# Order of the first loads, layout of the pool weights and turns of the memory rows in the opening of an eight-core decoder step

## The chip, the cores and the metric

The kernel runs on the 8 cores of one Trainium2 chip, every core with its own prompt sequence and 16 sample rows. The metric is the device time of the slowest core in microseconds (us). Some executions fall into a slower state, in which the cores of one die or both show a lower mean granted TensorE clock (in e1 a run of 1730.86 us with 0.93 to 0.94 on one die, and one of 1887.69 us with 0.93 to 0.95 on one and 0.84 to 0.85 on the other; 0.989 or more on every core in every fast run); only fast runs are compared. A ratio below is the mean time of one kernel's fast runs over that of the kernel before's fast runs of the same rounds, so it is not quite the ratio of the medians that stand beside it.

In this kernel TensorE (PE) does the matrix products into eight PSUM banks, VectorE (DVE), ScalarE (ACT) and GpSimd (POOL) the elementwise work. SyncE (SP) and GpSimd issue the loads, each on a queue of its own (59.24 and 84.08 MB on the page of the kernel before).

## The reference, cut to what matters

```python
def trunk(x, ...):                                   # DEPTH = 2
    for i in range(2):
        u = rmsnorm(x, g_mix[i])
        y = pool_mixer(u, ...) if i == 0 else conv_mixer(u, ...)
        x = x + y
        x = x + mem_attend(rmsnorm(x, g_attn[i]), mem_k[i], mem_v[i], w_q[i], w_o[i])
        x = x + sq_relu_mlp(rmsnorm(x, g_ffn[i]), w_up[i], w_down[i])
# pool_mixer: mean over a trailing window minus the token, one 256x256 product per group, a channel scale
# mem_kv: k, v = split(rmsnorm(mem, g_mem) @ w_kv)      256 memory rows per sequence
```

## The kernel before

The kernel keeps its own scheduler: operations are written in program order, each engine executes its own in that order, and semaphores come from the overlaps of buffers. The change sits in the `prelude`, the opening: it loads 16 blocks of x (128 rows, 512 KB each, seven buffers), applies the pool mixer and transposes x into the resident array `X`, and also turns the memory rows and multiplies them with w_k.

```python
xload(0); dma(SP, GV2, gv); xload(1)                       # SyncE's queue
dma(POOL, SCB, gv[R_PSCALE].broadcast_to([128, D]), "wpf") # GpSimd's queue: the pool scale on 128 partitions
dma(POOL, BANDS, bands)
for cc in range(2):
    dma(POOL, WPF[cc], w_pool[:, cc*128:(cc+1)*128, :].rearrange("g p e -> p g e"), "wpf")   # 1 KB rows
xload(2); dma(SP, MR, mem) ...; xload(3..6)
dma(POOL, SK, w_k); dma(POOL, SQ_, w_q)

def poolw():                                   # step 1
    8 x stt(WP(cc, g), WPF[cc](g), gain, SCB(g))              # VectorE, for the prompt
    2 x tt(WPS(cc), WPF[cc](), SCB(), mult, eng=POOL)         # GpSimd, a second copy for the samples
def stA(tb):  sum of squares of block tb on ACT; rstd; tsc(u, xrow(tb), rstd)   # normalise, DVE
def stB(tb):  window sums on PE; two copies out of PSUM, one on DVE, one on ACT
def stC(tb):  transpose of x and the pool product on PE; two copies into X
              if tb + 7 < 16: xload(tb + 7)               # SyncE: reuse of the buffer
def mem_turn(k):  one bank: 4 transposes; ACT copy, DVE copy, ACT copy, DVE copy of that bank
    if k == 3:
        dma(SP, memn, MEMN1)                              # spill of the turned memory rows
        dma(SP, GBC, gv[R_MIX].broadcast_to([128, D]))    # overwrites the bytes of MEMN1
# step s runs stB(s-1), stC(s-2), stA(s+1), then: poolw in step 1, mem_stats in step 2,
# mem_turn in steps 3 and 4, the four products rows(w_k) in steps 9 to 12
...
def attn_phase(l):
    bank_mod[0] = 7          # bank 7 is set aside; nxt() gives bank_ctr % bank_mod, the counter just goes on
```

The softmax here doesn't subtract the row's maximum and nothing guards it: scores larger than these inputs give would overflow.

## Time and profile before

| | us |
|---|---|
| time, median of 4 runs | 1642.3 (1640.96 to 1643.0) |
| opening, mean of the 8 cores | 101.1 (99.9 to 102.3) |
| rest, mean of the 8 cores | 1533.8 (1532.2 to 1535.1) |

"Opening" is read from the trace of each core: from the span's start to TensorE's transposes of the sample rows (16x16 f32). "Rest" is the span less the opening.

The page of the kernel before, slowest core (4): the span, TensorE's busy time, and the share of each engine in the chain that ended last.

```profile
span 1636.1 us, 28409 instructions; the slowest of 8 cores (1633.4 to 1636.1 us)
PE 1577.5 (96%) x10088; PEld 907.1 (55%) x10104; DVE 848.6 (52%) x1899; ACT 563.0 (34%) x1062; POOL 114.6 (7%) x245
PE 90%; DVE 3%; DMA 3%; ACT 2%; issue 2%; POOL 0%; DVEq 0%; ACTq 0%; SPq 0%; POOLq 0%
```

TensorE is nearly always busy, so what can be won lies where it is not. The chain of waits of the opening, same core (start, length, what):

```profile
3.56 17.97 DMA MEM<-w_pool
...
47.61 7.92 DMA memn<-MEM
55.59 0.33 SPq L354
56.08 10.31 DMA MEM<-x
```

There are two stalls on loads: for the pool weights until 21.5 us, and from 47.6 to 66.4 us for an x block whose issue stood in SyncE's queue behind the gain broadcast, which waited for the spill. The timeline between them (start, busy time, engine, line, operation, count):

```profile
21.62 7.42 DVE L327 SCALAR_TENSOR_TENSOR MEM<-MEM 128x256 bf16<-128x256 f32 x8 [1.43 <-DMA MEM<-w_pool]
21.68 5.11 POOL L331 TENSOR_TENSOR MEM<-MEM 128x1024 bf16<-128x1024 f32 x2 [15.54 <-DMA MEM<-w_pool]
```

The eight gain products and GpSimd's second copy run side by side.

The wait of 3.6 us ends at 990.6 us, where the second attention phase begins:

```profile
989.87 0.57 DVE L331 TENSOR_TENSOR MEM<-PS,MEM 128x400 bf16<-128x400 f32 x1
...
990.60 15.73 PE L292 MATMUL PS<-MEM 128*128 128x416 bf16 x75 [3.56 <-DVE MEM L331]
```

### The profile page before, as it was taken

How to read it: one execution, taken by the hardware profiler on the slowest of the kernel's cores; microseconds unless marked ns; L12 is line 12 of the kernel's file. 1: busy time of each engine (PE TensorE's matmuls, PEld its weight loads, DVE VectorE, ACT ScalarE, POOL GpSimd, SP SyncE). 2: the span in 40 equal slices, each digit the busy share in tenths (PEclk: the TensorE clock that was granted, in tenths of full speed). 3: DMA queues.
4: the chain of work that ended last, by engine and by line, in shares of the span. 5: the costliest groups of instructions: out<-in, count | busy, mean ns of one | idle time of the engine just before them, and what ended most of it. 6: DMA issues, size and time to landing. Idle time of an engine off the chain costs nothing.

```text
span 1636.1 us, 28409 instructions; the slowest of 8 cores (1633.4 to 1636.1 us)
## 1 busy us (share of the span) xinstructions
PE 1577.5 (96%) x10088; PEld 907.1 (55%) x10104; DVE 848.6 (52%) x1899; ACT 563.0 (34%) x1062; POOL 114.6 (7%) x245
## 2 busy tenths in 40 slices
PE   3899999999999999999999998999999999999997
PEld 3675555555555556555555554555555555555565
DVE  4566675555444344445666664676555444442235
ACT  3666344532111222222123223443652111213453
POOL 2002120110000000000000001120110000000000
PEclk9899999999999999999999999999999999999999
DMA  9859795675648617077000009694764773000012
GB/s 232 208 84 158 159 169 100 117 140 80 89 65 128 102 28 104 3 101 108 1 1 1 1 1 149 122 190 109 120 126 60 109 104 52 14 1 1 39 65 105
DMA packets 84565, 145.13 MB, mean 89 GB/s; under 512 B 4286, under 2 KB 37310, under 8 KB 84412
## 3 DMA queue, kind: packets, MB, share of 16 engines
q0 software_dynamic: 67568, 84.08, 38.0%
q1 hardware_dynamic: 16860, 59.24, 11.2%
q8 instruction: 84, 1.38, 0.3%
q14 instruction: 53, 0.43, 0.1%
HBM read 212.42 MB, written 14.36 MB: 139 GB/s over the span
## 4 chain that ended last, share of the span: by engine, by line
PE 90%; DVE 3%; DMA 3%; ACT 2%; issue 2%; POOL 0%; DVEq 0%; ACTq 0%; SPq 0%; POOLq 0%
PE PS L292 88%; DVE MEM L327 2%; PE PS L296 2%; ACT MEM L319 1%; DMA MEM<-w_pool 1%; PE PS L301 1%; DMA MEM<-x 1%; ACT MEM L308 1%; DMA memn<-MEM 0%; DVE MEM L345 0%; DVE MEM L331 0%; DMA y<-MEM 0%; DVE MEM L339 0%; ACT MEM L343 0%; POOL MEM L354 0%
## 5 line engine op out<-in xcount | busy, mean ns | idle before, releaser
L292 PE MATMUL PS<-MEM 128*128 128x416 bf16 (+7 forms) x9008 | 1502.0, 327 | 11.1 <-DVE MEM L331 4.6
L292 PEld LDWEIGHTS PS<-MEM 128*128 128x128 bf16 (+1 forms) x9024 | 837.2, 98 | 663.6 <-issue 44.0
L319 ACT ACTIVATE MEM<-PS 128x416 f32<-128x416 f32 (+5 forms) x469 | 238.7, 510 | 639.0 <-PE PS L292 628.4
L331 DVE TENSOR_TENSOR MEM<-PS,MEM 128x416 f32<-128x416 f32 (+6 forms) x533 | 297.5, 574 | 268.6 <-PE PS L292 260.5
L331 DVE TENSOR_TENSOR MEM<-MEM 128x416 bf16<-128x416 f32 (+3 forms) x282 | 159.8, 583 | 198.8 <-ACT MEM L319 190.3
L327 DVE SCALAR_TENSOR_TENSOR MEM<-MEM 128x416 bf16<-128x416 f32 (+7 forms) x322 | 181.1, 614 | 127.4 <-ACT MEM L319 102.1
L319 ACT ACTIVATE MEM<-MEM 128x416 bf16<-128x416 f32 (+9 forms) x299 | 185.1, 630 | 146.9 <-DVE MEM L331 112.2
L304 DVE SCALAR_TENSOR_TENSOR MEM<-MEM,PS 128x256 f32<-128x256 f32 x256 | 105.1, 420 | 72.6 <-PE PS L292 48.9
L296 PE MATMUL PS<-MEM 128*128 128x128 bf16 (+4 forms) x896 | 64.0, 252 | 26.8 <-DVE MEM L327 8.9
L343 ACT COPY MEM<-PS 128x512 f32<-128x512 f32 (+3 forms) x73 | 39.2, 537 | 130.9 <-PE PS L292 116.9
L296 PEld LDWEIGHTS PS<-MEM 128*128 128x128 bf16 (+2 forms) x896 | 51.2, 109 | 41.9 <-issue 40.3
L343 ACT CAST MEM<-PS 128x512 bf16<-128x512 f32 (+2 forms) x73 | 39.7, 556 | 65.9 <-PE PS L292 64.5
L345 DVE CAST MEM<-PS 128x512 bf16<-128x512 f32 (+1 forms) x68 | 43.8, 655 | 11.5 <-PE PS L292 11.3
L354 POOL DMA_DIRECT2D MEM<-cv x64 | 47.6, 744 | 13.8 <-PE PS L292 13.8
L319 ACT ACTIVATE PS<-PS 128x416 f32<-128x416 f32 (+3 forms) x67 | 33.1, 494 | 41.5 <-PE PS L292 41.2
L327 DVE SCALAR_TENSOR_TENSOR MEM<-PS,MEM 128x1024 f32<-128x1024 f32 (+1 forms) x17 | 21.8, 1282 | 44.9 <-ACT MEM L319 42.6
L351 POOL MEMSET MEM<- 128x4 bf16 (+1 forms) x96 | 15.0, 159 | 359.0 <-PE PS L296 271.7
L301 PE MATMUL PS<-MEM 128*128 128x128 f32 (+5 forms) x184 | 23.7, 268 | 14.3 <-DMA MEM<-gv 9.0
L339 DVE TENSOR_SCALAR MEM<-MEM 128x1024 bf16<-128x1024 f32 (+1 forms) x18 | 13.5, 753 | 32.9 <-ACT MEM L319 32.9
L354 POOL DMA_DIRECT2D MEM<-w_up x36 | 20.6, 581 | 137.9 <-PE PS L292 137.9
L301 PEld LDWEIGHTS PS<-MEM 128*128 128x128 f32 (+5 forms) x184 | 19.9, 139 | 16.9 <-issue 15.4
L354 POOL DMA_DIRECT2D MEM<-w_down x22 | 13.8, 636 | 201.9 <-PE PS L292 157.8
(28 smaller groups left out, 138.0 us busy)
## 6 DMA issues: line engine op xcount, KB each, us to landing
MEM<-ck SPq DMA_DIRECT2D x64, 512.0 KB, 6.9
MEM<-cv POOLq DMA_DIRECT2D x64, 256.0 KB, 6.7
MEM<-w_down POOLq DMA_DIRECT2D x6, 2048.0 KB, 18.1
MEM<-x SPq DMA_DIRECT2D x16, 512.0 KB, 11.5
MEM<-w_kv POOLq DMA_DIRECT2D x4, 2048.0 KB, 19.2
MEM<-w_o POOLq DMA_DIRECT2D x4, 2048.0 KB, 24.1
MEM<-w_up POOLq DMA_DIRECT2D x32, 256.0 KB, 12.7
MEM<-w_up POOLq DMA_DIRECT2D x4, 2048.0 KB, 17.8
```

The lines of the kernel that those rows point to most:

```text
L292: P.add(PE, "c", lambda e, o=out.ap, l=lhsT.ap, r=rhs.ap: e.matmul(out=o, lhsT=l, rhs=r, start=start, stop=stop), [lhsT, rhs], [out])
L296: P.add(PE, "c", lambda e, o=out.ap, l=lhsT.ap, r=rhs.ap: e.matmul(out=o, lhsT=l, rhs=r, start=start, stop=stop, is_transpose=is_transpose ...
L301: P.add(PE, "c", lambda e, o=out.ap, i=in_.ap, d=ident.ap: e.transpose(out=o, in_=i, identity=d), [in_, ident], [out])
L304: P.add(DVE, "c", lambda e, o=out.ap, a=in0.ap, b=in1.ap, c=acc.ap: e.scalar_tensor_tensor(out=o, in0=a, scalar=1.0, in1=b, op0=ALU.mult, ...
L308: P.add(ACT, "c", lambda e, o=out.ap, i=in_.ap, a=acc.ap: e.activation(out=o, in_=i, func=AF.Square, accum_out=a), [in_], [out, acc])
L319: P.add(ACT, "c", lambda e, o=out.ap, i=in_.ap: e.activation(out=o, in_=i, func=func, bias=bias, scale=sc), rd, [out])
L327: P.add(eng, "c", lambda e, o=out.ap, a=in0.ap, b=in1.ap: e.scalar_tensor_tensor(out=o, in0=a, scalar=sc, in1=b, op0=op0, op1=op1), rd, [out])
L331: P.add(eng, "c", lambda e, o=out.ap, a=in0.ap, b=in1.ap: e.tensor_tensor(out=o, in0=a, in1=b, op=op), [in0, in1], [out])
L343: P.add(ACT, "c", lambda e, o=out.ap, i=in_.ap: e.copy(out=o, in_=i), [in_], [out])
L345: P.add(eng, "c", lambda e, o=out.ap, i=in_.ap: e.tensor_copy(out=o, in_=i), [in_], [out])
L351: P.add(eng, "c", lambda e, o=out.ap: e.memset(o, val), [], [out])
L354: return P.add(q, "d", lambda e, o=out.ap, i=in_.ap: e.dma_start(out=o, in_=i), [in_], [out], chan=chan, after=after)
```

## The change

Its intent: the first microseconds carry only what is used first, no load waits behind another's spill (7.6 us of wait in SyncE's queue before), and ScalarE and VectorE do not wait for one bank (ScalarE waits 3.9 us, in four waits, for VectorE's copies before).

```diff
-wpool_d = din("w_pool", [4, 256, 256])
+wpool_d = din("w_pool", [2, 128, D])                     # laid out by the host: rows of 4 KB
-dma(POOL, SCB, scale row) first; bands; w_pool
+bands; w_pool in 4 KB rows; dma(POOL, SCB, scale row) last
+xload(3) ahead of the memory rows
-dma(POOL, SK, w_k); dma(POOL, SQ_, w_q)                  # at the start
+def weights():                                           # step 3, after stA(4)
+    dma(POOL, SK, w_k, after=(P.last[ACT],))
+def poolws():                                            # step 7, but next in GpSimd's own order
+    2 x tt(WPS(cc), WPF[cc](), SCB(), mult, eng=POOL); dma(POOL, SQ_, w_q); sample state
 stB:
-    second copy: eng=ACT
+    second copy: eng=ACT in odd blocks, DVE in even ones
 stC:
+    if tb == 11: dma(SP, GBC, gain row)                  # no longer behind the spill in mem_turn
-mem_turn(k): one bank, steps 3 and 4 (mem_stats in step 2)
+mem_turn(half): two banks, ACT on one while DVE is on the other, steps 4 and 5 (mem_stats in step 3)
-rows("wk0") in steps 9 to 12, their turns in 13 and 14
+rows("wk0") in steps 12 to 15, their turns in 16 and 17
 attn_phase:
+bank_ctr[0] = bank_ctr[0] % 8 % 7
 bank_mod[0] = 7
... (the sample rows scaled in place)
```

More of the change, by code (lines that the diff above doesn't have):

```diff
@@ L504, in prelude @@
         xload(1)
-        dma(POOL, SCB(), DV(gv_d[R_PSCALE:R_PSCALE + 1, :].broadcast_to([128, D])), "wpf")
         dma(POOL, BANDS(), DV(bands_d), "wp")
         for cc in range(2):
-            dma(POOL, WPF[cc](), DV(wpool_d[:, cc * 128:(cc + 1) * 128, :].rearrange("g p e -> p g e")), "wpf")
+            dma(POOL, WPF[cc](), DV(wpool_d[cc].rearrange("p (g e) -> p g e", g=4)), "wpf")
+        dma(POOL, SCB(), DV(gv_d[R_PSCALE:R_PSCALE + 1, :].broadcast_to([128, D])), "wpf")
         xload(2)
+        xload(3)
         for nb in range(2):
             dma(SP, MR[nb](), DV(mem_d[nb * 128:(nb + 1) * 128, :]), "mr")
-        for tb in range(3, NXB):
+        for tb in range(4, NXB):
             xload(tb)
-        dma(POOL, SK(), DV(wsrc_sq(wsrc["wk0"])), f"w{slot_of['wk0']}")
-        dma(POOL, SQ_(), DV(wsrc_sq(wsrc["wq0"])), f"w{slot_of['wq0']}")
         cp(IDB(), IDF())
@@ L527, in poolw @@
                     stt(WP(cc, g), WPF[cc](g), G(2 * g + cc, sl(R_MIX, R_MIX + 1)), SCB(g), ALU.mult, ALU.mult)
+        def weights():
+            dma(POOL, SK(), DV(wsrc_sq(wsrc["wk0"])), f"w{slot_of['wk0']}", after=(P.last[ACT],))
+        def poolws():
             for cc in range(2):
                 tt(WPS(cc), WPF[cc](), SCB(), ALU.mult, eng=POOL)
+            dma(POOL, SQ_(), DV(wsrc_sq(wsrc["wq0"])), f"w{slot_of['wq0']}")
             for i in range(2):
@@ L559, in stB @@
             for half in range(2):
-                cp(PLB[tb % 2](sl(half * 4, half * 4 + 4)), PSr(bks[half], "p (j t) -> p j t", j=4), eng=(ACT if half else DVE))
+                cp(PLB[tb % 2](sl(half * 4, half * 4 + 4)), PSr(bks[half], "p (j t) -> p j t", j=4), eng=(ACT if half and tb % 2 else DVE))
         def stC(tb):
@@ L578, in stC @@
                 xload(tb + NXB)
-            if tb == 10:
+            if tb == 11:
+                dma(SP, GBC(), DV(gv_d[R_MIX:R_MIX + 1, :].broadcast_to([128, D])), "gbc")
                 dma(SP, XSR(p=(0, NS)), DV(xs_d), "xsr")
@@ L589, in mem_stats, with mem_turn @@
                 tsc(MR[nb](), MR[nb](), st_(2, 16 + nb), ALU.mult)
-        def mem_turn(k):
-            bk = nxt()
-            for j in range(2):
-                c = 2 * k + j
-                for nb in range(2):
-                    tp(PSv(bk, j * 256 + nb * 128, j * 256 + (nb + 1) * 128), MR[nb](sl(c * 128, (c + 1) * 128)), IDF())
-            for j in range(2):
-                c = 2 * k + j
-                act(MEMN(c), PSv(bk, j * 256, (j + 1) * 256), AF.Copy, scale=G(c, sl(R_MEM, R_MEM + 1)))
-                tsc(MEMN1(c), PSv(bk, j * 256, (j + 1) * 256), G(c, sl(R_MEM + 1, R_MEM + 2)), ALU.mult)
-            if k == 3:
+        def mem_turn(half):
+            bks = [nxt(), nxt()]
+            for i in range(2):
+                for j in range(2):
+                    c = 4 * half + 2 * i + j
+                    for nb in range(2):
+                        tp(PSv(bks[i], j * 256 + nb * 128, j * 256 + (nb + 1) * 128), MR[nb](sl(c * 128, (c + 1) * 128)), IDF())
+            for i in range(2):
+                for j in range(2):
+                    c = 4 * half + 2 * i + j
+                    act(MEMN(c), PSv(bks[i], j * 256, (j + 1) * 256), AF.Copy, scale=G(c, sl(R_MEM, R_MEM + 1)))
+                for j in range(2):
+                    c = 4 * half + 2 * (1 - i) + j
+                    tsc(MEMN1(c), PSv(bks[1 - i], j * 256, (j + 1) * 256), G(c, sl(R_MEM + 1, R_MEM + 2)), ALU.mult)
+            if half == 1:
                 spill.append(dma(SP, DV(memn_d), V(MEMN1.ap.rearrange("p c n -> p (c n)"), MEMN1().ivs), "spill"))
-                dma(SP, GBC(), DV(gv_d[R_MIX:R_MIX + 1, :].broadcast_to([128, D])), "gbc")
         st_ctr = [0]
@@ L661, in samples_a @@
             rstd(18, P16)
-            stt(UF(p=P16), XSR(p=P16), st_(2, 18, P16), GBC(p=P16), ALU.mult, ALU.mult)
-            cp(UCB(p=P16), UF(p=P16))
-            dma(SP, DV(nps_d[:, 14, :]), UF(p=P16), "ucf")
+            stt(XSR(p=P16), XSR(p=P16), st_(2, 18, P16), GBC(p=P16), ALU.mult, ALU.mult)
+            cp(UCB(p=P16), XSR(p=P16))
+            dma(SP, DV(nps_d[:, 14, :]), XSR(p=P16), "ucf")
         def samples_b():
@@ L691, in prelude @@
         extra[1] = [poolw]
-        extra[2] = [mem_stats]
-        extra[3] = [lambda: mem_turn(0), lambda: mem_turn(1)]
-        extra[4] = [lambda: mem_turn(2), lambda: mem_turn(3)]
+        extra[3] = [weights, mem_stats]
+        extra[4] = [lambda: mem_turn(0)]
+        extra[5] = [lambda: mem_turn(1)]
+        extra[7] = [poolws]
         for i, a in enumerate(quad):
-            extra[9 + i].append(lambda a=a: rows("wk0", mk_d, *a))
+            extra[12 + i].append(lambda a=a: rows("wk0", mk_d, *a))
         for i, a in enumerate(quad):
-            extra[13 + i // 2].append(lambda a=a: turn(*a))
+            extra[16 + i // 2].append(lambda a=a: turn(*a))
         extra[11].append(lambda: norm_a(0, BUF[0], parts=2))
@@ L1455 @@
         "gv": gv, "ident": np.eye(128, dtype=np.float32), "bands": _make_bands(),
-        "w_pool": f(w_pool)[0], "w_conv_in": f(w_conv_in)[0], "w_conv_out": f(w_conv_out)[0],
+        "w_pool": f(f(w_pool)[0].reshape(4, 2, 128, 256).transpose(1, 2, 0, 3).reshape(2, 128, D)), "w_conv_in": f(w_conv_in)[0], "w_conv_out": f(w_conv_out)[0],
         "w_q": f(w_q), "w_qT": f(np.swapaxes(np.asarray(w_q), 1, 2)), "w_kv": f(w_kv), "w_o": f(w_o), "w_up": f(w_up), "w_down": f(w_down),
```

## The prediction

> **What bounds the kernel now.** The page: span 1636.1 us, TensorE busy 96%, matmuls 90% of the chain that ended last. From 101.5 us on (timeline, core 4; about 100.5 to 103 on the eight cores) TensorE is nearly always busy, so everything after that instant should only shift. The change touches what lies before it, the opening, where TensorE is busy for about 65 of 101 us. The chain of waits there shows three stalls:
> 1. 3.6 to 21.6 us: waiting for w_pool. Its two DMAs land 15 and 18 us after issue, sharing the DMA engines with x, the memory rows, w_k and w_q. The 16 engines are busy without a gap from about 3 to 72 us.
> 2. 21.6 to 29 us: the eight 128x256 gain products take 994 ns each on VectorE while GpSimd makes its second copy (2 x 2573 ns). VectorE's 128x416 form takes 644 ns, a 1024-wide one 1283 ns; from these I estimate 480 ns without company. [...]
> 3. 47.6 to 66.5 us: the DMA queue of SyncE waits 7.9 us for the spill of memn, because the gain broadcast behind it overwrites the same bytes; x blocks 10 to 14 sit behind, and ScalarE idles 6.6 us until block 10 lands (60 to 66.5 us).
> Besides, the memory transposes' copies alternate between ScalarE and VectorE on one bank: steps 3 and 4 take 12.4 us for two, where later steps take 2.6 to 4.
>
> **What the change does.**
> - Holding w_k (and w_q behind it), 4 KB rows, and the broadcast last: the first 20 us carry only what is used first. I estimate w_pool and its scale landing near 16 to 17 us instead of 21.6, the products done near 20 instead of 29: about 8 us.
> - Second copy after w_k's issue: included above. It then slows VectorE for 5 us near 26 to 31 us, where ScalarE is the limit: at most 1 us.
> - Gain broadcast issued after block 11: stall 3 goes, 6 us.
> - Two-bank memory turns: about 3 us.
> - Pool copies of even blocks moved to VectorE: ScalarE loses 0.58 us in every second step where it is the limit: about 2 us.
> Against this, the weights start near 25 us instead of 5. w_kv alone takes 18.7 us to land later in the trace, w_q the same; with the x blocks beside them I expect w_k near 50 to 53 us (first use moved to step 12, near 58) and w_q near 70 to 80, against first use near 82. So the margin for w_q is thin and may eat 0 to 4 us.
>
> **Sum.** 8 + 6 + 3 + 2 - 1 = 18, all on the chain, none given back later: continuous TensorE work starts near 83 us. 1642.4 - 18.4 = **1624 us**, range **1617 to 1632**. That is 1.1%: faster by over 2% 0.01, within 2% 0.98, slower 0.01.
>
> **What would show it.** First gain product near 17 us, each near 0.48 us; no wait of x loads on memn; w_k landing before its rows need it; TensorE continuous from 80 to 88 us; equal span from there to the end (about 1534 us).
>
> **What would make it wrong.** (a) w_q not landed when the weight transposes begin: the chain shows a wait on w_q and the gain shrinks to 10 to 14. (b) x blocks 7 to 15 land late while they share the engines with w_k and w_q: ScalarE waits on x in steps 6 to 12. (c) SyncE and GpSimd loads share the engines evenly, so the pool loads come no earlier than now. (d) w_v, issued earlier, collides with w_q's tail.

The sum: it came to 18 us (8 + 6 + 3 + 2 - 1), and the author took 18.4 us off.

## More of the kernel before

Last, who TensorE waited for after the opening (total us, times, longest):

```profile
PE PS L292 <- DVE MEM L331: 4.6, 2, 3.6
PE PS L301 <- DVE MEM L331: 4.5, 2, 3.3
```

## The result, and the profile after

The kernel after takes 1626.1 us (median of 4 runs, 1625.64 to 1626.76) against 1642.3; the ratio is 0.9903, 95% interval 0.9885 to 0.992. That is within 2%, inside the predicted range and 2 us from the predicted time. Its inner parts, however, are not the predicted ones:

| mean of 8 cores, us | before | after | difference | predicted |
|---|---|---|---|---|
| opening | 101.1 | 92.4 | 8.7 | 18.4 |
| rest | 1533.8 | 1529.1 | 4.7 | 0 |

The opening won half of what was forecast, and a place that the prediction had called untouched won 4.7 us. The two sum to 13.4 us here. The mean core span over all fast runs of a later set on one chip (the rounds of e9) fell by 14.8 us (1635.8 to 1621.0), the slowest core's by 15.5.

The page after, slowest core (5):

```profile
span 1624.3 us, 28431 instructions; the slowest of 8 cores (1618.2 to 1624.3 us)
PE 1575.0 (97%) x10104; PEld 906.3 (56%) x10104; DVE 854.2 (53%) x1907; ACT 560.8 (35%) x1054; POOL 113.9 (7%) x245
PE 92%; DVE 2%; ACT 2%; DMA 2%; issue 2%; POOL 0%; DVEq 0%; ACTq 0%; SPq 0%; POOLq 0%
```

The chain of the opening after (the scale row is `gv`):

```profile
3.31 16.70 DMA MEM<-gv
...
47.22 13.68 DMA MEM<-x
...
72.33 2.46 PE PS L296 x40
74.79 1.73 PE PS L292 x8
76.52 2.46 PE PS L296 x40
78.97 1.73 PE PS L292 x8
```

The first stall is still there, only that it is the scale that lands last, at 20.0 us. The wait for memn is gone, but x is still waited for, until 60.9 us. At the end each step is TensorE's own: 40 products of a block and 8 of a memory row, 4.2 us together. The timeline of the part between:

```profile
20.10 3.26 DVE L327 SCALAR_TENSOR_TENSOR MEM<-MEM 128x256 bf16<-128x256 f32 x8 [1.60 <-DMA MEM<-gv]
29.62 0.90 POOL L354 DMA_DIRECT2D MEM<-w_kv  x1 [25.76 <-ACT MEM L319]
30.52 4.66 POOL L331 TENSOR_TENSOR MEM<-MEM 128x1024 bf16<-128x1024 f32 x2
30.86 5.86 DVE L339 TENSOR_SCALAR MEM<-MEM 128x1024 f32<-128x1024 f32 x2 [0.88 <-ACT MEM L319]
35.89 0.45 PE L301 MATMUL PS<-MEM 128*128 128x128 f32 x1 [5.81 <-DVE MEM L339]
```

The gain products now take 3.26 us instead of 7.42. But GpSimd's second copy meets the normalisation of the memory rows: two VectorE instructions take 5.86 us, and TensorE waits 5.81 us for them. The waits of TensorE after the opening:

```profile
PE PS L301 <- DVE MEM L331: 2.4, 1, 2.4
PE PS L292 <- DVE MEM L331: 2.0, 2, 1.0
```

Where the opening's time was won and lost shows when ScalarE starts on each x block (mean of 8 cores, us, from the traces):

| block | 3 | 5 | 6 | 7 | 9 | 10 | 11 | 13 | 15 | sample transposes |
|---|---|---|---|---|---|---|---|---|---|---|
| before | 28.4 | 40.7 | 46.7 | 49.3 | 54.9 | 66.8 | 69.9 | 80.7 | 88.0 | 101.1 |
| after | 23.5 | 33.4 | 41.9 | 47.5 | 52.6 | 55.1 | 60.0 | 69.5 | 76.9 | 92.4 |
| won so far | 4.9 | 7.3 | 4.8 | 1.8 | 2.3 | 11.7 | 9.9 | 11.2 | 11.1 | 8.7 |

Some 5 us are won by block 3. Block 5's lead of 7.3 us flatters, for before had started its memory turns by then; when both kernels have them behind (blocks 7 to 9) only about 2 us are left. Then before meets its stall and the lead becomes 11.7 us, and 3 us of that are lost again toward the end.

### The profile page after: what moved, and what is told of

Same layout as the page of the kernel before. It is cut to its first block, busy times and chain, and to the rows that moved or that the text cites. A ratio compares the mean times of both kernels' runs of the same rounds, so it can differ in the third digit from the quotient of the medians.

```text
span 1624.3 us, 28431 instructions; the slowest of 8 cores (1618.2 to 1624.3 us)
## 1 busy us (share of the span) xinstructions
PE 1575.0 (97%) x10104; PEld 906.3 (56%) x10104; DVE 854.2 (53%) x1907; ACT 560.8 (35%) x1054; POOL 113.9 (7%) x245
## 4 chain that ended last, share of the span: by engine, by line
PE 92%; DVE 2%; ACT 2%; DMA 2%; issue 2%; POOL 0%; DVEq 0%; ACTq 0%; SPq 0%; POOLq 0%
PE PS L292 89%; PE PS L296 2%; DVE MEM L327 1%; ACT MEM L319 1%; PE PS L301 1%; DMA MEM<-gv 1%; DMA MEM<-x 1%; ACT MEM L308 1%; DVE MEM L331 0%; DVE MEM L345 0%; DVE MEM L339 0%; POOL MEM L354 0%; ACT MEM L343 0%; DVEq L1389 0%; ACTq L1389 0%
## 5 line engine op out<-in xcount | busy, mean ns | idle before, releaser
L292 PE MATMUL PS<-MEM 128*128 128x416 bf16 (+7 forms) x9024 | 1501.3, 327 | 8.3 <-DVE MEM L345 2.7
L292 PEld LDWEIGHTS PS<-MEM 128*128 128x128 bf16 (+1 forms) x9024 | 837.3, 98 | 659.8 <-issue 38.5
L327 DVE SCALAR_TENSOR_TENSOR MEM<-MEM 128x416 bf16<-128x416 f32 (+7 forms) x322 | 176.9, 601 | 126.9 <-ACT MEM L319 108.5
L296 PEld LDWEIGHTS PS<-MEM 128*128 128x128 bf16 (+2 forms) x896 | 49.2, 107 | 30.2 <-issue 28.6
L343 ACT CAST MEM<-PS 128x512 bf16<-128x512 f32 (+2 forms) x65 | 35.2, 554 | 68.0 <-PE PS L292 67.3
L345 DVE CAST MEM<-PS 128x512 bf16<-128x512 f32 (+1 forms) x76 | 48.5, 658 | 11.7 <-PE PS L292 11.7
L354 POOL DMA_DIRECT2D MEM<-cv x64 | 47.7, 745 | 13.4 <-PE PS L292 13.4
L301 PE MATMUL PS<-MEM 128*128 128x128 f32 (+5 forms) x184 | 25.0, 277 | 18.3 <-DMA MEM<-gv 8.4
L339 DVE TENSOR_SCALAR MEM<-MEM 128x1024 bf16<-128x1024 f32 (+1 forms) x18 | 17.9, 997 | 24.0 <-ACT MEM L319 24.0
L354 POOL DMA_DIRECT2D MEM<-w_up x36 | 20.6, 582 | 132.5 <-PE PS L292 132.5
## 6 DMA issues: line engine op xcount, KB each, us to landing
MEM<-w_down POOLq DMA_DIRECT2D x6, 2048.0 KB, 17.7
MEM<-w_up POOLq DMA_DIRECT2D x4, 2048.0 KB, 17.1
```

The source lines that it names most:

```text
L292: P.add(PE, "c", lambda e, o=out.ap, l=lhsT.ap, r=rhs.ap: e.matmul(out=o, lhsT=l, rhs=r, start=start, stop=stop), [lhsT, rhs], [out])
L296: P.add(PE, "c", lambda e, o=out.ap, l=lhsT.ap, r=rhs.ap: e.matmul(out=o, lhsT=l, rhs=r, start=start, stop=stop, is_transpose=is_transpose ...
L301: P.add(PE, "c", lambda e, o=out.ap, i=in_.ap, d=ident.ap: e.transpose(out=o, in_=i, identity=d), [in_, ident], [out])
L327: P.add(eng, "c", lambda e, o=out.ap, a=in0.ap, b=in1.ap: e.scalar_tensor_tensor(out=o, in0=a, scalar=sc, in1=b, op0=op0, op1=op1), rd, [out])
L339: P.add(eng, "c", lambda e, o=out.ap, a=in0.ap: e.tensor_scalar(out=o, in0=a, scalar1=sc, scalar2=None, op0=op0), rd, [out])
L343: P.add(ACT, "c", lambda e, o=out.ap, i=in_.ap: e.copy(out=o, in_=i), [in_], [out])
```

## The experiments

Theory: (1) the opening's gain comes mostly from taking the gain row out of SyncE's queue; (2) what the earlier gain products won was lost again to GpSimd's copy in its new place; (3) the rest's gain is the line on the bank counter. Rivals: the hold of the weights or the 4 KB rows make the gain; the rest moved because traffic or clock did. Every kernel gave correct results.

| run | kernel | opening | rest | median of the fast runs (fast of all) | ratio to before | mean span against before |
|---|---|---|---|---|---|---|
| e1 | before again | 100.9 | 1534.1 | 1639.59 (2 of 4) | 0.9996 | +0.1 |
| e2 | before, bank line alone | 101.4 | 1529.4 | 1635.00 (3 of 4) | 0.9969 | -4.0 |
| e3 | after, second copy late | 87.0 | 1529.3 | 1620.46 (2 of 4) | 0.9879 | -18.3 |
| e4 | after, rows in steps 9 to 12 | 91.8 | 1528.5 | 1623.63 (3 of 4) | 0.9898 | -14.9 |
| e5 | e3 without the hold | 89.3 | 1528.9 | 1622.64 (3 of 4) | 0.9887 | -17.1 |
| e6 | after, 1 KB rows | 92.9 | 1529.2 | 1625.37 (4 of 4) | 0.9910 | -13.2 |
| e7 | after, gain row behind the spill | 100.7 | 1529.1 | 1633.97 (3 of 5) | 0.9964 | -4.9 |
| e8 | e3, scale by TensorE, first form | 88.7 | 1529.5 | 1621.81 (4 of 4) | 0.9889 | -16.4 |
| e9 | after again | 91.3 | 1529.3 | 1624.10 (4 of 4) | 0.9905 | -14.8 |
| e10 | e3, one-bank turns | 88.0 | 1529.4 | 1622.25 (3 of 4) | 0.9889 | -17.7 |
| e11 | e3, pool copies on ScalarE | 88.7 | 1529.4 | 1622.05 (3 of 4) | 0.9891 | -17.4 |
| e12 | e3, scale by TensorE, mended | 85.3 | 1529.7 | 1617.87 (4 of 4) | 0.9863 | -21.0 |

The 95% intervals of the ratios are about 0.002 to either side. Opening and rest come from one profiled execution each. The last column uses every fast run instead: the mean span of all cores, less that of before in the same rounds, with a standard error of 0.3 to 0.7 us. It is a check on the openings.

### e1 and e9: the two kernels again

> The kernel before, unchanged, to see how far one of its profiled executions lies from another. Two lengths are read from every profile, as means of the eight cores: the opening (from the span's start to TensorE's transposes of the sample rows, 16x16 f32) and the rest (from there to the span's end). First profiles: before 101.1 + 1533.8 us, after 92.4 + 1529.1. If the first profile of before was an ordinary one, opening 101 and rest 1534 within 1 us, and a time near 1638 to 1642.

> The kernel after, unchanged, on the same chip as the three runs beside it: opening 92.4 and rest 1529.1 again within 1 us, ratio to before 0.990 to 0.992.

The openings came out at 100.9 (101.1 before) and 91.3 (92.4): one profiled execution is known to about 1 us (e9 lies just outside the 1 us that was expected), and differences below that are not settled by one run. Two of e1's runs were slow (1730.86 and 1887.69 us) and are not used.

### e2: the bank line alone

```diff
 def attn_phase(l):
+    bank_ctr[0] = bank_ctr[0] % 8 % 7
     bank_mod[0] = 7
```

> The kernel before with one line of the change alone, the one that carries the PSUM bank rotation over into the attention phases. Theory: this line, which the change's summary does not name, gives the 4.4 us that the rest lost, all at the start of the second attention phase, where banks 3 to 6 were reused out of turn: opening 101 as before, rest 1529.4, ratio to before near 0.997. Rival: the rest got shorter because the earlier loads shifted DMA traffic or the granted clock; then the rest stays at 1534.

The rest fell to 1529.4, the whole of it, with the opening as before. TensorE's waits after the opening, slowest core:

```profile
PE PS L301 <- DVE MEM L331: 3.2, 1, 3.2
...
PE PS L292 <- DVE MEM L331: 2.0, 2, 1.0
```

The 3.6 us wait on the product L292 has shrunk to 1.0 us, on all eight cores. The counter explains it: at the second attention phase it stands at 815 in the program of the kernel before. The conv phase counts modulo 8 and has just used banks 1 to 6 for its last two channel groups. 815 modulo 7 is 3, so the next banks are 3 to 6, among them the bank that the last VectorE product of the conv phase still reads: TensorE stops until that product ends (989.87 + 0.57 us, TensorE resumes at 990.60). 815 modulo 8 is 7, and modulo 7 that is 0, so with the line banks 0, 1 and 2 come first, which were free. At the first attention phase both formulas give bank 1, and nothing changes there. The rival falls: loads were not touched in e2. The clock did take part, but together with the wait: e2, where the wait is 1.0 us, has no stretch at 0.50 there. Core 4 in the 5.7 us after it, before and then e2 (stretch, length, busy time of PE, PEld, DVE, ACT and POOL, granted clock, DMA share, GB/s):

```profile
990.60:996.30 5.70, 5.70 (x17) 2.45 (x18) 0.00 (x1) 0.52 (x1) 0.00 (x0) 0.50 1.02 139
992.40:998.10 5.70, 5.70 (x36) 3.27 (x35) 2.40 (x5) 0.00 (x0) 0.00 (x0) 1.00 1.07 147
```

TensorE did 17 products in before where e2 did 36. The granted clock fell to 0.50 around this wait for 3.4 or 6.8 us on seven cores of before and six of e1, and on none of e2. So 2.6 of the 4.4 us are the wait itself; from the 4.3 us at 0.50 (mean of before's eight cores) I estimate that the slow products after it cost most of the rest.

### e3: the second copy late

```diff
-tt(WPS(cc), WPF[cc](), SCB(), ALU.mult, eng=POOL)      # right behind w_k's issue
+tt(WPS(cc), WPF[cc](), SCB(), ALU.mult)                # VectorE, step 9; w_q right behind w_k
```

> The kernel after, with the second copy of the pool weights made by VectorE in step 9 instead of by GpSimd right behind w_k's issue (w_q then issued right behind w_k). Theory: GpSimd's two products (4.66 us) block the two normalisations of the memory rows on VectorE (5.86 us for two, against 0.75 each), and the memory transposes wait for them: the two take 0.75 us each again, opening 3 to 5 us shorter than in after (88 to 89 us), rest unchanged at 1529. Rival: ScalarE's order sets the pace there and the wait is hidden: opening 92 within 1 us.

The opening fell to 87.0, by 4.3 to 5.4 us against the two runs of after; by the mean span it is 3.5 us (18.3 less 14.8). The two normalisations of the memory rows, timeline of the slowest core, first in before and then in e3:

```profile
33.03 0.75 DVE L339 TENSOR_SCALAR MEM<-MEM 128x1024 f32<-128x1024 f32 x1 [0.88 <-ACT MEM L319]
34.59 0.75 DVE L339 TENSOR_SCALAR MEM<-MEM 128x1024 f32<-128x1024 f32 x1 [0.81 <-ACT MEM L319]
...
31.35 1.06 DVE L339 TENSOR_SCALAR MEM<-MEM 128x1024 f32<-128x1024 f32 x1 [0.88 <-ACT MEM L319]
32.55 0.30 PE L301 MATMUL PS<-MEM 128*128 128x128 f32 x1 [1.98 <-DVE MEM L339]
32.91 0.75 DVE L339 TENSOR_SCALAR MEM<-MEM 128x1024 f32<-128x1024 f32 x1 [0.50 <-ACT MEM L319]
```

The change had moved the contention, not removed it. In these traces the normalisation lasts about as long as GpSimd's two products beside it (4.66 us on the slowest core): on all eight cores of after the first normalisation begins 0.3 us after GpSimd's first product, takes 4.9 us and ends 0.6 us after GpSimd's second; it takes 0.75 us in before and 1.06 us in e3. TensorE's wait for it falls from 5.8 to 2.0 us. e3 also issues w_q 5 us earlier (30.2 instead of 35.3 us), but w_q lands at nearly the same time (75.0 instead of 75.6), and the lead over after is already 3.8 us at block 6 (38.1 instead of 41.9), right behind the first memory turn.

### e4: the w_k rows early

```diff
-extra[12 + i].append(rows("wk0"))
+extra[9 + i].append(rows("wk0"))        # turns in steps 13 and 14
```

> The kernel after, with the w_k rows back in steps 9 to 12 (and their turns in 13 and 14), where before has them. Theory: in after each of the four rows (1.9 us on TensorE) falls in a step in which TensorE is the limit (steps of 4.2 us), while in before two of them ran in the wait for x; w_k has landed near 54 us, before step 9 near 58 us, so they fit again: opening 2 to 4 us shorter than in after (88.5 to 90.5), rest unchanged. Rival: w_k lands too late for step 9 on some cores and ScalarE waits behind it: opening equal or longer (92 or more).

Neither came: 91.8 is after's opening within the run-to-run difference. ScalarE's two waits for x fell from 2.1 and 1.7 us to 0.3 and 0.1, for the steps before were longer. Block 15 started at 78.2 us (76.9 in after) and the way from there to the sample transposes took 13.6 us instead of 15.5. So it only redistributes the work. What holds the last steps once the rows are gone from them was not isolated.

### e5: the hold undone

```diff
-dma(POOL, SK(), w_k, after=(P.last[ACT],))    # step 3
+dma(POOL, SK(), w_k)                          # behind the scale row, at the start; w_q behind it
```

> The kernel of e3 (after, second copy late on VectorE; opening 87.0) with w_k and w_q issued at once behind the scale row instead of being held until x block 4 has been normalised: the hold alone is undone. Theory A, that the hold makes the early loads fast: scale lands at 22 us or later instead of 20, opening 91 or more. Theory B, that the hold does little for the first stall, as w_k stands behind bands, w_pool and scale in its own queue anyway, and only x and the memory rows feel it: scale within 1 us of 20, x blocks 4 to 8 later, w_q earlier and x blocks 11 to 15 with it; opening within 2 us of 87.

The scale landed at 19.3 us, as with the hold (19.2 in e3): theory A falls, for the pool weights and the scale stand ahead of w_k in the same queue. But x block 4 landed at 29.5 us instead of 23.7, and ScalarE waited 2.4 us for it. The opening is 2.3 us longer, a little more than theory B allowed, but only 1.2 us by the mean span, so the size is not settled. Blocks 11 to 15 did not come earlier, as theory B had it, though w_q did (67.9 instead of 75.0): block 15 landed at 71.2 us instead of 69.9. What the hold buys is the early landing of x: block 4 by 5.8 us.

### e6: rows of 1 KB

```diff
-dma(POOL, WPF[cc](), w_pool in 128 rows of 4 KB)
+dma(POOL, WPF[cc](), w_pool in 512 rows of 1 KB)
```

> The kernel after with w_pool read in 1 KB rows, as before: 512 pieces a half instead of 128. Theory: the small rows make the pool weights and the scale behind them land later, scale at 22 instead of 20 (in before the two halves came 3.5 and 4.8 us apart, in after 2.9 and 3.6), opening 94 to 95 instead of 92.4. Rival: bytes count and not rows, and the pool weights come no later: opening within 1 us of 92.4.

The scale landed at 21.0 us instead of 19.6 (19.4 in e9), but the opening is 92.9: 0.5 to 1.6 us longer than in the two runs of after. The scale is later by 1.5 us (22 was expected), the second half of w_pool itself by 0.5 us (16.7 instead of 16.2); the effect on the opening is too small to be settled here.

### e7: the gain row behind the spill again

```diff
 mem_turn: spill
+    dma(SP, GBC, gain row)
 stC: if tb == 11:
-    dma(SP, GBC, gain row)
```

> The kernel after with the load of the mixer gain behind the spill of memn again, ahead of the x blocks. Theory: the queue waits some 8 us for the spill to land (47 to 55 us), x blocks 12 and later are issued that much later, ScalarE waits for them: opening 4 to 7 us longer than in after (96 to 99). Rival: the DMA engines are full there anyway with w_q, and x blocks land at their pace of one in 3.5 us: opening less than 2 us longer.

The opening became 100.7, longer by 8.3 to 9.4 us, more than expected, and is as long as before's. The chain of the slowest core has the old stall again:

```profile
46.36 8.07 DMA memn<-MEM
54.97 14.24 DMA MEM<-x
```

Block 11 was issued at 55.5 us instead of 47.1 and landed at 68.1 instead of 59.9 (means of 8 cores), so landing follows issue here and the rival falls. This run tells the most: with this one part undone, what the other parts win in the opening is nearly gone. The wait at block 11 cuts the lead over before to 1.7 us (68.2 against 69.9), and the 2.9 us of lead at block 15 (85.1 against 88.0) are lost in the last steps.

### e8 and e12: the scale made on the core

The scale is a row repeated on 128 partitions, 512 KB, and lands last (at 19.6 us in after). Two fp32 TensorE products with a one-row selector spread it from the gain rows, which land at 8 us. The eight gain products moved ahead of block 2's normalisation. In e8 the selector was made behind block 1's normalisation; in e12 it is made as soon as the identity is there.

```diff
-dma(POOL, SCB(), scale row broadcast to 128 partitions, "wpf")
+cp(sel, IDF[0:13, 9:10] broadcast)          # e12: at the start; e8: inside scale_rows, in step 0
+def scale_rows(): for half: mm(bank, sel, GV2[:, half]); cp(SCB half, bank, eng=ACT)
+scale_rows() behind stA(0) (e8: behind gains), poolw() ahead of stA(2)
```

> The kernel of e3 with the pool scale no longer loaded as 128 copies of a row (landing at 20 us, 4 us behind w_pool) but spread over the partitions by two TensorE products from the gain rows that land at 8 us, and the eight gain products moved ahead of block 2's normalisation. If the scale's landing holds up the first pool products: first gain product near 16 us instead of 20, opening 83 to 85 instead of 87.0, time 3 to 4 us under e3 (near 1616). If x blocks set the pace later anyway: first product early, opening 86 or more.

> The kernel of e8 mended: there the two TensorE products that spread the scale (3.75 us in fp32) stood behind VectorE's normalisation of block 1 and ahead of the first pool products. Here their selector is made at once and they run as soon as the gain rows land at 8 us. First gain product at 16.5 to 17.5 us (19.4 in e3, 21.0 in e8), opening 83.5 to 85.5, time under e3's: ratio to before 0.986 to 0.988. If x blocks pace the later steps, opening 86 to 87 as in e3.

e8 failed: its first gain product came at 21.0 us, later than e3's 19.4. Its products waited for VectorE and then held TensorE:

```profile
15.23 3.75 PE L292 MATMUL PS<-MEM 13*128 13x512 f32 x4 [6.62 <-DVE MEM L345]
```

In e12 the first gain product comes at 16.8 us (mean of 8 cores; 17.08 on the slowest):

```profile
17.08 3.25 DVE L327 SCALAR_TENSOR_TENSOR MEM<-MEM 128x256 bf16<-128x256 f32 x8
```

e12 takes 1617.87 us against 1624.10 of after on the same chip and 1640.56 of before: the fastest. Of the 2.6 us that its gain products come earlier than in e3, 1.7 reach the opening's end (85.3, inside what was expected); by the mean span it is 2.6 us. What the scale's new source and the earlier place of the gain products give singly was not separated.

### e10 and e11: one-bank turns, and pool copies on ScalarE

```diff
-mem_turn(half): two banks          +mem_turn(k): one bank, two groups a step      # e10
-eng=(ACT if half and tb % 2 else DVE)   +eng=(ACT if half else DVE)               # e11
```

> The kernel of e3 (opening 87.0) with the memory transposes' copies on one bank at a time again, two groups in step 4 and two in step 5. Theory: ScalarE and VectorE wait for one another's copies on the shared bank, about 1 us per group: opening 2 to 4 us longer (89 to 91). Rival: the steps are paced by something else and the order of the copies costs nothing: opening within 1 us of 87.0.

> The kernel of e3 (opening 87.0) with the second half of every pooled block copied by ScalarE again, not by VectorE in even blocks. Theory of the prediction: ScalarE (0.58 us a copy) is the limit in the steps up to 9: opening 1.5 to 2.5 us longer (88.5 to 89.5). Rival: from step 9 on x's landing and TensorE set the pace, so that what ScalarE loses before is waited for anyway: opening within 1 us of 87.0.

e10 is 1.0 us longer than e3, the rival's side, and not separable from no effect with one run (0.6 us by the mean span). e11 is 1.7 us longer, as the prediction had it, but 0.9 us by the mean span, so its size is not settled either.

## Why the prediction was right or wrong

The time was right, but as a sum of errors that cancelled, and so by luck: the opening gave 8.7 us of the 18.4, and 4.7 us came from a line that the prediction did not count. Point by point:

- **First stall, predicted 8 us, measured 5.0.** The gain products ended at 23.0 instead of 28.0 us (means of 8 cores). The step that failed is "w_pool and its scale landing near 16 to 17 us": the second half of w_pool did land at 16.2, but the scale behind it at 19.6. Before, the last of the three had landed at 20.5. Holding w_k did not help them, as e5 shows (scale at 19.3 us without the hold, 19.2 with it); the outcome of the prediction's own doubt (c), pool loads no earlier than before, was nearly what happened. How evenly the queues shared was measured on one core of after alone: of the packets that started from 3 to 20 us, GpSimd's queue had 576 (1.79 MB) and SyncE's 678 (2.45 MB). Of the 5.0 us, 0.8 are the earlier start (19.8 instead of 20.6) and 4.2 the products without GpSimd beside them. That half of the term was right: the estimate was 480 ns a product, and one takes 480 ns (mean of the eight on the slowest core; they overlap a little, so eight take 3.26 us).
- **Second copy, predicted "at most 1 us", measured 4.3 to 5.4 us (e3; 3.5 by the mean span).** With the first stall this is the largest error in the opening. The prediction reasoned that ScalarE is the limit there, and did not ask which VectorE instructions would fall beside the copy: the two that the memory transposes wait for.
- **Gain row, predicted 6 us, measured 8.3 to 9.4 (e7).** Right in mechanism, sized too small, because the prediction took ScalarE's idle time on one core (6.6 us; 9.2 is the mean of the eight) as all that could be won.
- **Two-bank turns, predicted 3 us, measured 1.0 (e10).** The long steps were only partly due to the bank: from block 5 to block 7 it takes 11.6 us in e10 and still 10.9 in e3 (32.9 to 43.8). In e3 the chain of the slowest core runs over TensorE's own products there, and its granted clock is 0.50 from 34 to 40 us.
- **Pool copies, predicted 2 us, measured 1.7 (e11; 0.9 by the mean span).** Of the right kind; the size is not settled.
- **The weights.** w_k landed at 51.9 us and w_q at 75.6, both inside the forecast (50 to 53, 70 to 80), and no wait on either shows in the chain. But the doubt (b) came true: ScalarE waits 2.1 and 1.7 us for blocks 11 and 12. In these traces x lands more slowly while w_q is under way: blocks 11 to 15 land about 3.7 us apart beside w_q (59.9, 63.8, 67.3, 71.1, 74.5), and in before, with w_q landed at 60.2, blocks 10 to 14 land about 1.5 us apart (66.7, 68.4, 69.9, 71.3, 72.5). On the slowest core of after, from 64 to 74 us, GpSimd's queue moved 467 packets and SyncE's 388, and SyncE got 138 GB/s; in before, alone from 66 to 73 us, it got 306 GB/s.
- **The w_k rows.** The prediction did not count that they move to steps that TensorE fills (4.2 us a step). e4 shows that this cost nothing net.
- **"Everything after that instant should only shift": failed.** The rest lost 4.7 us, and e2 shows that one line does it, which the change's few words do not name and the prediction passed over, though the diff has it.

The single terms do not add up to the opening's gain (8.3 + 2.3 + 1.7 + 1.0 alone is 13.3, and 9 were won), and they should not: each was measured with the others in place, and a later wait hides an earlier gain. What stays open is the share of the 4 KB rows, of the hold, of the two-bank turns and of the pool copies, all near the 1 us between two executions, and what holds the last steps in e4. The new place of the scale row and of block 3's load was not undone singly. A later issue of w_q, to let x blocks 11 and 12 land sooner, was not tried.

## What to carry to other kernels

When a contending instruction is moved, list what will run beside it in its new place; the move gave back on the memory rows (4.3 to 5.4 us, e3) about what it had won on the gain products (4.2 us). A load that waits for a store must not stand in the queue ahead of loads that wait for nothing: here it was the largest term (8.3 to 9.4 us, e7), and it hid nearly all the gains before it (opening of e7 100.7 us, of before 101.1). A wait of TensorE can cost more than its own length: here one of 3.6 us was followed, on core 4, by 5.7 us of products at a granted clock of 0.50. Where a rotating buffer counter changes its modulus, check that the next buffers are the longest unused ones, and read every line of a diff, also those that its summary leaves out.

## What else the traces show of loads and of the clock

- A load beside a load on the other queue: beside w_q, block 11 took 12.8 us from issue to landing (47.1 to 59.9, means of the 8 cores of after), with 512 KB of spill issued 0.5 us ahead of it.
- The stretches at a granted clock of 0.50 in the opening (before and after) and at the second attention phase (before) last 3.4, 6.8 or 10.2 us, and the 40 products of a block take 4.72 us there instead of 2.62 (at 63.8 us in the kernel after, slowest core, where the stretch runs from 62.9 to 69.8 us and TensorE had waited 3.12 us). In e3 the clock fell on all eight cores between 30 and 35 us, next to a wait of 1.7 to 2.0 us, the longest from 28 us on. Over whole executions the mean granted clock of every core was 0.989 or more in every fast run; only slow runs fell below (0.93 to 0.95 on one die and 0.84 to 0.85 on the other in the run of 1887.69 us).
- The case of e2, a rotation over the PSUM banks whose modulus changes between phases, so that a bank still being read comes up too early, cost 4.4 us here.
